# Last residual of the first half in tiles of its own, half of layer 1's v in products of 512 columns, and the last product with final_g by VectorE

## The chip, the cores and the metric

The kernel runs on one core of one Trainium2 chip. The metric is the device time of one launch in microseconds (us), the median of several runs. The engines are PE (TensorE: matrix products), ACT (ScalarE), DVE (VectorE), POOL (GpSimd) and SP (SyncE, whose queue issues all the transfers here). Each engine works through its own queue in order; an instruction waits until what it needs is done, and all that stands behind it on that engine waits with it.

## The reference

A trunk of two layers over 1024 tokens of 1024 channels, in fp32. Layer 0 has two mixers (a recurrent one, a, and a chunked attention, b), whose gated outputs go through one output projection; layer 1 has a gated product in which v is normalized over its channels and mixed over positions.

```python
def even_layer(h, ...):                       # layer 0
    p = rmsnorm(h, g) @ w_in
    ...
    y_a = rwkv7_mix(...) * silu(gate_a)       # 512 channels
    y_b = chunk_attention(...) * silu(gate_b) # 512 channels
    return h + concatenate([y_a, y_b]) @ w_out

def spatial_gating(u, v, ...):
    mu, var = mean(v), mean(square(v - mu))   # over the 1024 channels of a token
    v = (v - mu) * rsqrt(var + LN_EPS) * ln_g + ln_b
    sv = einsum('gij,bnjgc->bnigc', w, v in blocks of 128 tokens) + sg_b
    return u * sv

def odd_layer(h, ...):                        # layer 1
    u, v, gate = split(rmsnorm(h, g) @ w_in)  # 1024 columns each
    y = spatial_gating(gelu(u), gelu(v), ...)
    return h + (y * silu(gate)) @ w_out

def reference(x, ...):
    return rmsnorm(odd_layer(even_layer(x)), final_g)
```

## The kernel before

Every fp32 product is made of three products of rounded parts: an operand is cast to a high part (ACT) and the rest is subtracted out as a low part (POOL or DVE); `mm3_steps` then issues high × high (L256), high × low or low × high (L258), and the third (L260) for each of 8 (or 4) blocks of 128 contracted channels. Names with h or H are high parts, with l or L low ones. Tokens come in 8 blocks t of 128.

The program is written in one order and a scheduler, which simulates the engines, chooses from it the order of each engine's queue; buffers of a pool come round under a tag, and an instruction that takes a buffer again waits until its last reader is done.

Three places matter.

- **The output projection of layer 0** (`out_steps`, L1115). For a block t it loads y (`yraw`, L1123), casts it to `yh` (ACT, L1126), subtracts `yl` (L1127, DVE or POOL), and for each half n of 512 columns multiplies into one of two accumulators `acc` and adds the residual (DVE, L1142). It is made in two halves. The first, over `ya_d`, is in `fill_steps` and is fed between the steps of the attention: its residual is x, loaded into one of three buffers under the tag `res` (L1135), and the sum is stored in `hp_d` (L1167). The second, over `yb_d`, starts when the attention is done: for t = 0 the residual is `hp_d`, loaded through the same three `res` buffers; for later t it comes in `ht` (L1204). `wh` and `wl` of L222 and L225 are the first weights of layer 1, cast and subtracted meanwhile.
- **v of layer 1** (L1229 to L1241). v has 1024 columns in four blocks cb of 256. For each cb and t one product `accv` of 128 tokens × 256 columns (24 matmuls, with `xH2`, `xL2`, the normalized input, as the stationary operand) is evicted by ACT through gelu into `vp[cb][:, t]` (L1240), with its sum in `sv`. Behind it the mean `mu` is formed (DVE), 32 squares `junk` on ACT (L1263) give the variance, a reciprocal root of 8 columns on DVE follows (L72 to L85), then `v_norm` (L1274), the cast `vh` (ACT, L1289), the rest `vl` (POOL, L1290), and the products `psv` with the position weights (L1308, L1309). Meanwhile PE makes `accu` and `accg`, the u and gate products of layer 1. The weights of the output projection of layer 1, `WHL`, are loaded (L1112), cast (ACT, L1113) and subtracted (L1114) wherever the scheduler places them.
- **The end** (L1318 to L1355): for each t the output projection of layer 1, the sum of squares of each half (`junk`, ACT, L1341), `hg` = h × final_g for each half (POOL, L1342), the mean `v` (DVE, L1344), the reciprocal root (`rsqa`, `rstd`), the scaling of one half by DVE (L1347) and of the other by ACT (L1348), and the store.

Of the kernel before, what the change touches and what calls it, by code (L numbers as in the profile page):

```python
# [8 lines left out]
F32 = mybir.dt.float32  # L9
F32R = mybir.dt.float32r  # L10
I32 = mybir.dt.int32
BF16 = mybir.dt.bfloat16
AF = mybir.ActivationFunctionType
ALU = mybir.AluOpType
# [4 lines left out]
P = 128  # L19
T = 1024  # L20
D = 1024
KO = 8
# [41 lines left out]
def f32(ap):  # L64
    return ap.bitcast(F32)
# [34 lines left out]
def trunk_kernel(  # L100
# [4 lines left out]
    nc = tc.nc  # L105
    x = x[0]
# [90 lines left out]
    ya_d = dtile("ya_d", [NPAIR, P, T])  # L197
# [66 lines left out]
    def mm3(*args):  # L264
        run(mm3_steps(*args))
# [12 lines left out]
    ps_acc = pa.enter_context(tc.tile_pool(name="ps_acc", bufs=2, space=PSUM))  # L278
# [260 lines left out]
    for p in range(NPAIR):  # L539
# [23 lines left out]
        for hf in range(2):  # L563
            tsl = slice(hf * 512, hf * 512 + 512)
            psl = slice(p * P, p * P + P)
            r, k, v = rT[hf], kT[hf], vT[hf]
# [549 lines left out]
    def out_steps(t, ps_o, src, k0, parts, resid, ht, hp, yp, yb_, hi=nc.scalar.copy, lo=nc.vector):  # L1116

        tok = slice(t * P, t * P + P)
        yh, yl = [], []
        k1 = 0  # L1120
        for i, nk in enumerate(parts):
            raw = yp.tile([P, nk, P], F32, tag=f"yraw{i}", name="yraw", bufs=yb_)
            nc.sync.dma_start(raw, src[k1:k1 + nk, :, tok].rearrange("k p c -> p k c"))  # L1123
            h_ = yp.tile([P, nk, P], F32R, tag=f"yh{i}", name="yh", bufs=yb_)
            l_ = yp.tile([P, nk, P], F32R, tag=f"yl{i}", name="yl", bufs=yb_)
            hi(h_, raw)  # L1126
            lo.tensor_tensor(l_, raw, f32(h_), op=ALU.subtract)  # L1127
            yh += [h_[:, k] for k in range(nk)]
            yl += [l_[:, k] for k in range(nk)]
            k1 += nk  # L1130
        for n in range(2):
            ns = slice(512 * n, 512 * n + 512)
            if resid is not None:
                xt = hp.tile([P, 512], F32, tag="res", name="res", bufs=3)
                nc.sync.dma_start(xt, resid(t)[:, ns])  # L1135
            else:
                xt = ht[n]
            ps = ps_o.tile([P, 512], F32, tag="acc", name="acc")
            yield from mm3_steps(ps, lambda k: yh[k], lambda k: yl[k],
                                 lambda k: W[k0 + k][0][:, ns], lambda k: W[k0 + k][1][:, ns], k1)  # L1140
            ht[n] = xt if ht[n] is None else ht[n]
            nc.vector.tensor_tensor(ht[n], ps, xt, op=ALU.add)  # L1142
            yield
# [6 lines left out]
    def fill_steps():  # L1150

        nonlocal op
        yield from early
        pw.close()
        pf_.close()
        for k in range(KO):
            place_wout(xp, f"x{k}")
        op = po_.enter_context(tc.tile_pool(name="op", bufs=1, side="right"))
        yeng = (nc.gpsimd.tensor_copy if YP else nc.scalar.copy, nc.gpsimd if YP else nc.vector)
        weng = (nc.gpsimd.tensor_copy if WP else nc.scalar.copy, nc.gpsimd)  # L1160
        for c in range(4):
            load_wout(op, w_out_e[0], c, 2, *weng)
        for t in range(8):
            ht = [None, None]
            yield from out_steps(t, ps_acc, ya_d, 0, [4], lambda t: x[t * P:(t + 1) * P, :], ht, op, op, 2, *yeng)
            for n in range(2):
                nc.sync.dma_start(hp_d[t][:, 512 * n:512 * n + 512], ht[n])  # L1167
            if t < 4:
                load_wout(op, w_out_e[0], 4 + t, 2, *weng)

    op = None
# [22 lines left out]
    wpv = ExitStack()  # L1194
# [31 lines left out]


    sv = lp.tile([P, 4, 8], F32, name="sv")
    for c2 in range(2):  # L1229
        ws = [wv.pop() if wv else load_w(wvs[i], w_in_o[0], 1024 + 256 * (2 * c2 + i), n=256, bufs=1, rp=wvs[0])  # L1230
              for i in range(2)]
        for i, t4 in [(0, 0), (1, 0), (0, 1), (1, 1)]:
            cb = 2 * c2 + i
            wh, wl = ws[i]
            for t in range(4 * t4, 4 * t4 + 4):
                ts_ = slice(t * P, t * P + P)
                ps = ps_v.tile([P, 256], F32, tag="acc", name="accv")
                mm3(ps, lambda k: xH2[k][:, ts_], lambda k: xL2[k][:, ts_],
                    lambda k: wh[:, k, :], lambda k: wl[:, k, :])
                nc.scalar.activation(vp[cb][:, t], ps, AF.Gelu_apprx_tanh,  # L1240
                                     accum_out=sv[:, cb, t:t + 1])  # L1241
    wpv.close()
    lq = ctx.enter_context(tc.tile_pool(name="lq", bufs=1, side="right", reuse_waits="tile"))
    Rb = lq.tile([P, 8, P], F32, name="Rb")
# [82 lines left out]
    with tc.tile_pool(name="op1", bufs=1, reuse_waits="tile") as op:  # L1327
        fg = op.tile([P, D], F32, name="fg")
        nc.sync.dma_start(fg, final_g.unsqueeze(0).to_broadcast([P, D]))
        for t in range(8):  # L1330
# [5 lines left out]
            for n in range(2):  # L1336
                ns = slice(512 * n, 512 * n + 512)
                for _ in range(3 * KO):
                    next(steps)
                junk = op.tile([P, 512], BF16, tag="junk", name="junk", bufs=2)  # L1340
                nc.scalar.activation(junk, ht[:, ns], AF.Square, scale=D ** -0.5, accum_out=ms[:, n:n + 1])  # L1341
                nc.gpsimd.tensor_tensor(hg[:, ns], ht[:, ns], fg[:, ns], op=ALU.mult)  # L1342
            v = op.tile([P, 1], F32, tag="v", name="v", bufs=2)
            nc.vector.scalar_tensor_tensor(v, ms[:, 0:1], 1e-6, ms[:, 1:2], op0=ALU.add, op1=ALU.add)  # L1344
            rstd = op.tile([P, 1], F32, tag="rstd", name="rstd", bufs=2)
# [41 lines left out]
```

## Time and profile before

| | us |
|---|---|
| median of three runs | 1177.39 (1175.95, 1177.39, 1180.84) |
| the profiled execution | 1180.27, at a mean granted clock of 0.974 |
| its span in the trace | 1178.6 |
| PE busy | 1119.8 (95%) |
| DVE / ACT / POOL busy | 622.6 / 469.0 / 432.0 |
| bytes moved | 156.39 MB, mean 133 GB/s |

A row of the timeline is: start, length, engine, line, operation, output <- input, shape, and in brackets how long the engine had stood idle before it and what ended that. "x2" means two instructions in one row. A row of the chain is: start, length, what. Times in rows are counted from the start of the span. A matmul's length in a row is from its start until it has drained; the next one starts earlier than that, so the distance of two starts is what a matmul costs PE.

### The profile page before, as it was taken

How to read it: one execution, taken by the hardware profiler on the slowest of the kernel's cores; microseconds unless marked ns; L12 is line 12 of the kernel's file. 1: busy time of each engine (PE TensorE's matmuls, PEld its weight loads, DVE VectorE, ACT ScalarE, POOL GpSimd, SP SyncE). 2: the span in 40 equal slices, each digit the busy share in tenths (PEclk: the TensorE clock that was granted, in tenths of full speed). 3: DMA queues.
4: the chain of work that ended last, by engine and by line, in shares of the span. 5: the costliest groups of instructions: out<-in, count | busy, mean ns of one | idle time of the engine just before them, and what ended most of it. 6: DMA issues, size and time to landing. Idle time of an engine off the chain costs nothing.

```text
span 1178.6 us, 21117 instructions
## 1 busy us (share of the span) xinstructions
PE 1119.8 (95%) x8162; PEld 929.2 (79%) x8162; DVE 622.6 (53%) x1276; ACT 469.0 (40%) x1008; POOL 432.0 (37%) x448
## 2 busy tenths in 40 slices
PE   8999999998899898999997899899999999999997
PEld 5788778787777676767886778789998888888886
DVE  6455656456585867634687767464100753333433
ACT  5554554430322232312675646234417232231432
POOL 4345545361223433423322463311402464351222
PEclk9999999995999998999999899999999999999999
DMA  6124446469322533293587784862401232122541
GB/s 209 39 81 143 116 117 164 140 205 193 109 83 83 161 101 100 73 215 118 162 227 184 222 264 147 270 216 90 134 10 55 87 110 72 63 88 89 166 133 71
DMA packets 169125, 156.39 MB, mean 133 GB/s; under 512 B 25257, under 2 KB 138562, under 8 KB 168898
## 3 DMA queue, kind: packets, MB, share of 16 engines
q1 hardware_dynamic: 169026, 155.06, 44.9%
q8 instruction: 64, 1.05, 0.4%
q14 instruction: 35, 0.29, 0.1%
HBM read 102.02 MB, written 53.00 MB: 132 GB/s over the span
## 4 chain that ended last, share of the span: by engine, by line
PE 58%; DMA 7%; DVE 5%; ACT 1%; issue 1%; POOL 1%; SPq 0%; DVEq 0%; ACTq 0%; POOLq 0%
PE acc L256 8%; PE acc L258 8%; PE acc L260 8%; PE accv L256 3%; PE accv L260 3%; PE accv L258 3%; PE accu L256 3%; PE accu L260 2%; PE accg L260 2%; PE accu L258 2%; PE accg L258 2%; PE accg L256 2%; PE st L1069 2%; DMA wraw<-in_w_out_e_dram 2%; PE psx L770 1%; PE psg L713 1%
## 5 line engine op out<-in xcount | busy, mean ns | idle before, releaser
L256 PE MATMUL acc<-xH,wh 128*128 128x512 f32 x528 | 214.7, 407 | 1.6 <-DVE rT L422 0.6
L258 PE MATMUL acc<-xL,wh 128*128 128x512 f32 x528 | 213.5, 405 | 0.0
L225 POOL TENSOR_TENSOR wl<-wraw,wh 128x512 fp32r<-128x512 f32 (+1 forms) x106 | 148.9, 1424 | 175.4 <-ACT wh L222 160.0
L260 PE MATMUL acc<-xH,wl 128*128 128x512 f32 x528 | 212.0, 401 | 0.0
L256 PEld LDWEIGHTS acc<-xH,wh 128*128 128x128 f32 x528 | 101.5, 192 | 23.6 <-DVE rT L422 1.0
L258 PEld LDWEIGHTS acc<-xL,wh 128*128 128x128 f32 x528 | 101.2, 192 | 21.2 <-issue 0.9
L260 PEld LDWEIGHTS acc<-xH,wl 128*128 128x128 f32 x528 | 101.0, 191 | 21.2
L256 PE MATMUL acc<-WHL,yh 128*128 128x512 f32 x256 | 101.9, 398 | 4.5 <-DVE res L1142 3.4
L222 ACT CAST wh<-wraw 128x512 fp32r<-128x512 f32 (+1 forms) x102 | 62.7, 653 | 108.5 <-PE acc L258 43.3
L258 PE MATMUL acc<-WHL,yh 128*128 128x512 f32 x256 | 100.8, 394 | 0.0
L260 PE MATMUL acc<-WHL,yl 128*128 128x512 f32 x256 | 100.8, 394 | 0.0
L256 PE MATMUL accv<-wh,xH 128*128 128x256 f32 x256 | 71.7, 283 | 0.0
L258 PE MATMUL accv<-wl,xH 128*128 128x256 f32 x256 | 71.7, 283 | 0.0
L260 PE MATMUL accv<-wh,xL 128*128 128x256 f32 x256 | 71.4, 285 | 0.0
L256 PEld LDWEIGHTS acc<-WHL,yh 128*128 128x128 f32 x256 | 48.4, 189 | 15.6 <-DVE res L1142 4.1
L258 PEld LDWEIGHTS acc<-WHL,yh 128*128 128x128 f32 x256 | 48.3, 189 | 9.6 <-POOL WHL L1114 0.2
L260 PEld LDWEIGHTS acc<-WHL,yl 128*128 128x128 f32 x256 | 48.1, 188 | 9.7
L256 PE MATMUL accu<-xH,wh 128*128 128x512 f32 x128 | 50.5, 395 | 0.0
L260 PE MATMUL accu<-xH,wl 128*128 128x512 f32 x128 | 49.9, 390 | 0.0
L258 PE MATMUL accu<-xL,wh 128*128 128x512 f32 x128 | 49.9, 390 | 0.0
L260 PE MATMUL accg<-xH,wl 128*128 128x512 f32 x128 | 49.9, 389 | 0.0
L256 PE MATMUL accg<-xH,wh 128*128 128x512 f32 x128 | 49.8, 389 | 0.0
(433 smaller groups left out, 2438.0 us busy)
## 6 DMA issues: line engine op xcount, KB each, us to landing
wraw<-in_w_in_e_dram SPq DMA_DIRECT2D x66, 256.0 KB
wraw<-in_w_in_o_dram SPq DMA_DIRECT2D x32, 256.0 KB
xt<-in_x_dram SPq DMA_DIRECT2D x8, 512.0 KB
ar_d<-ar SPq DMA_DIRECT2D x8, 512.0 KB
q_d<-hl SPq DMA_DIRECT2D x8, 512.0 KB
bk<-bk_d SPq DMA_DIRECT2D x8, 512.0 KB
ag<-ar_d SPq DMA_DIRECT2D x16, 256.0 KB
k_d<-hl SPq DMA_DIRECT2D x8, 512.0 KB
```

The costliest lines, as they stand in the source:

```text
L222: c_ = hi(wh[:, ks], raw)
L225: nc.gpsimd.tensor_tensor(wl[:, ks], raw, f32(wh[:, ks]), op=ALU.subtract)
L256: fill(nc.tensor.matmul(ps, lhsT=ah(k), rhs=bh(k), start=(k == 0), stop=False), k == 0)
L258: fill(nc.tensor.matmul(ps, lhsT=ah(k), rhs=bl(k), start=False, stop=False), False)
L260: fill(nc.tensor.matmul(ps, lhsT=al(k), rhs=bh(k), start=False, stop=(k == nk - 1)), False)
L713: nc.tensor.matmul(psg[h][:, 2 * j + i], lhsT=bk[hss[h], 2 * pj + j, i, :], rhs=ag[hss[h], h, 2 * pj + j, i, :], start=True, stop=True)
L770: nc.tensor.matmul(ps[t_, i], lhsT=lhsT(f, i), rhs=rhs[f[0], i], start=True, stop=True)
L1069: nc.tensor.transpose(st[:, o:o + P], pfs[j][:, k0:k0 + P], ident)
```

## The change

It has three parts.

1. The two residual halves of t = 7 of the first half get buffers of their own (`res7`), under the tag `wraw` of the pool `op`, in which the raw output weights lay; they are loaded ahead of t = 5. The other residuals keep the three `res` buffers.
2. The second half of v (columns 512 to 1023 of v) is made in products of 512 columns: its weights lie in `wh2` and `wl2`, loaded in four pieces through the same raw buffers, and one product fills a whole accumulator, which ACT evicts in two pieces of 256. The first half of v stays in products of 256.
3. For t = 7 and n = 1 the product with final_g is made by DVE.

Where the order of the queues differs: DVE around the residuals of t = 7 (in the order's names `res_7967` and `res_7969` are the new tiles). Before, from the sum of t = 6 to that of the second half's t = 0:

```order
L1142 TENSOR_TENSOR res<-acc,res 128x512
L1083 TENSOR_TENSOR yb<-po,lo 64x512
L1142 TENSOR_TENSOR res<-acc,res 128x512 x2
L1127 TENSOR_TENSOR yl<-yraw,yh 128x512
L1142 TENSOR_TENSOR res<-acc,res 128x512 x2
L1127 TENSOR_TENSOR yl<-yraw,yh 128x512
L1142 TENSOR_TENSOR ht<-acc,res 128x512 x2
```

and in the changed kernel:

```order
L1145 TENSOR_TENSOR res<-acc,res 128x512
L1083 TENSOR_TENSOR yb<-po,lo 64x512
L1145 TENSOR_TENSOR res<-acc,res 128x512 x2
L1127 TENSOR_TENSOR yl<-yraw,yh 128x512
L1145 TENSOR_TENSOR res_7967<-acc,res_7967 128x512
L1145 TENSOR_TENSOR res_7969<-acc,res_7969 128x512
L1127 TENSOR_TENSOR yl<-yraw,yh 128x512
L1145 TENSOR_TENSOR ht<-acc,res 128x512 x2
```

The order is the same; only the two adds of t = 7 read other tiles. On SP the residual loads moved. Before, from the store of t = 5's second half on (`hp_d_132` is t = 0, `hp_d_139` t = 7):

```order
L1167 DMA hp_d_137<-res 128x512
L1135 DMA res<-in_x_dram 128x512
L1094 DMA yb_d<-yb 128x512
L1167 DMA hp_d_138<-res 128x512
L1123 DMA yraw<-yb_d 128x4x128
L221 DMA wraw<-in_w_in_o_dram 128x4x256 x2
L1167 DMA hp_d_138<-res 128x512
L1135 DMA res<-in_x_dram 128x512
L1123 DMA yraw<-yb_d 128x4x128
L1167 DMA hp_d_139<-res 128x512
L1135 DMA res<-hp_d_132 128x512
L221 DMA wraw<-in_w_in_o_dram 128x4x256
```

In the changed kernel the two loads of t = 7 stand some 20 rows earlier,

```order
L1175 DMA hp_d_135<-res 128x512
L1123 DMA yraw<-ya_d 128x4x128
L1172 DMA res_7967<-in_x_dram 128x512
L1172 DMA res_7969<-in_x_dram 128x512
L1175 DMA hp_d_135<-res 128x512
L1138 DMA res<-in_x_dram 128x512
L1123 DMA yraw<-ya_d 128x4x128
L990 DMA rd<-rr 4x128
L1138 DMA res<-in_x_dram 128x512
```

and at the place of before:

```order
L1175 DMA hp_d_137<-res 128x512
L1138 DMA res<-hp_d_132 128x512
L1094 DMA yb_d<-yb 128x512
L1175 DMA hp_d_138<-res 128x512
L1123 DMA yraw<-yb_d 128x4x128
L221 DMA wraw<-in_w_in_o_dram 128x4x256 x2
L1175 DMA hp_d_138<-res 128x512
L1138 DMA res<-hp_d_132 128x512
L1123 DMA yraw<-yb_d 128x4x128
L1175 DMA hp_d_139<-res_7967 128x512
L1175 DMA hp_d_139<-res_7969 128x512
```

The two residual loads of the second half (`res<-hp_d_132`) have moved up by one place each in the turn of the `res` buffers.

On ACT the casts of the output weights of layer 1 moved. Before, from the middle of v to the squares (`vp,sv<-accv` are the evictions of v):

```order
L1113 CAST WHL<-wraw 128x1024
L1240 ACTIVATE vp,sv<-accv 128x256 x2
L222 CAST wh<-wraw 128x1024 x2
L1113 CAST WHL<-wraw 128x1024
L1240 ACTIVATE vp,sv<-accv 128x256 x4
L222 CAST wh<-wraw 128x1024 x2
L1240 ACTIVATE vp,sv<-accv 128x256 x12
L222 CAST wh<-wraw 128x512 x2
L1240 ACTIVATE vp,sv<-accv 128x256 x2
L222 CAST wh<-wraw 128x512 x2
L1240 ACTIVATE vp,sv<-accv 128x256 x2
L1263 ACTIVATE junk,va_9745<-vp,mu 128x256 x10
```

and, at the end of v and in the squares, in the changed kernel:

```order
L1244 ACTIVATE vp,sv<-accv 128x256 x16
L1286 ACTIVATE junk,va_9547<-vp,mu 128x256 x4
L1113 CAST WHL<-wraw 128x1024
L1286 ACTIVATE junk,va_9547<-vp,mu 128x256 x2
L1113 CAST WHL<-wraw 128x1024
L1286 ACTIVATE junk,va_9547<-vp,mu 128x256
L1320 ACTIVATE y<-accu 128x512
L1286 ACTIVATE junk,va_9547<-vp,mu 128x256 x6
L1113 CAST WHL<-wraw 128x1024
L1286 ACTIVATE junk,va_9547<-vp,mu 128x256 x2
L1325 ACTIVATE th<-accg 128x512
L1286 ACTIVATE junk,va_9547<-vp,mu 128x256 x7
```

Before, three casts of WHL stood among the evictions of v and none among the 32 squares; now three stand among the squares. In the place of the former stand the casts of `wh2`. The load that they need on SP is issued behind a wait for the last product of v, because the new `wl2` lies where the raw output weights will. On PE the first `psv` stands 161 matmuls behind the last of v, where it stood 141 behind.

At the end DVE has one instruction more, the product of L1365, between the last add (L1145) and the mean `v` (L1368); on POOL 15 products with final_g are left of 16.

```diff
--- before.py
+++ after.py
@@ -1131,8 +1131,11 @@
         for n in range(2):
             ns = slice(512 * n, 512 * n + 512)
             if resid is not None:
-                xt = hp.tile([P, 512], F32, tag="res", name="res", bufs=3)
-                nc.sync.dma_start(xt, resid(t)[:, ns])
+                if isinstance(resid(t), list):
+                    xt = resid(t)[n]
+                else:
+                    xt = hp.tile([P, 512], F32, tag="res", name="res", bufs=3)
+                    nc.sync.dma_start(xt, resid(t)[:, ns])
             else:
                 xt = ht[n]
             ps = ps_o.tile([P, 512], F32, tag="acc", name="acc")
@@ -1160,9 +1163,14 @@
         weng = (nc.gpsimd.tensor_copy if WP else nc.scalar.copy, nc.gpsimd)
         for c in range(4):
             load_wout(op, w_out_e[0], c, 2, *weng)
+        res7 = []
         for t in range(8):
             ht = [None, None]
-            yield from out_steps(t, ps_acc, ya_d, 0, [4], lambda t: x[t * P:(t + 1) * P, :], ht, op, op, 2, *yeng)
+            if t == 5:
+                for n in range(2):
+                    res7.append(op.tile([P, 512], F32, tag="wraw", name="res7", bufs=2))
+                    nc.sync.dma_start(res7[n], x[7 * P:8 * P, 512 * n:512 * n + 512])
+            yield from out_steps(t, ps_acc, ya_d, 0, [4], lambda t: res7 if t == 7 else x[t * P:(t + 1) * P, :], ht, op, op, 2, *yeng)
             for n in range(2):
                 nc.sync.dma_start(hp_d[t][:, 512 * n:512 * n + 512], ht[n])
             if t < 4:
@@ -1226,19 +1234,34 @@
 
 
     sv = lp.tile([P, 4, 8], F32, name="sv")
-    for c2 in range(2):
-        ws = [wv.pop() if wv else load_w(wvs[i], w_in_o[0], 1024 + 256 * (2 * c2 + i), n=256, bufs=1, rp=wvs[0])
-              for i in range(2)]
-        for i, t4 in [(0, 0), (1, 0), (0, 1), (1, 1)]:
-            cb = 2 * c2 + i
-            wh, wl = ws[i]
-            for t in range(4 * t4, 4 * t4 + 4):
-                ts_ = slice(t * P, t * P + P)
-                ps = ps_v.tile([P, 256], F32, tag="acc", name="accv")
-                mm3(ps, lambda k: xH2[k][:, ts_], lambda k: xL2[k][:, ts_],
-                    lambda k: wh[:, k, :], lambda k: wl[:, k, :])
-                nc.scalar.activation(vp[cb][:, t], ps, AF.Gelu_apprx_tanh,
-                                     accum_out=sv[:, cb, t:t + 1])
+    def v_block(cb, n, t, wh, wl):
+
+        ts_ = slice(t * P, t * P + P)
+        ps = ps_v.tile([P, n * 256], F32, tag="acc", name="accv")
+        mm3(ps, lambda k: xH2[k][:, ts_], lambda k: xL2[k][:, ts_],
+            lambda k: wh[:, k, :], lambda k: wl[:, k, :])
+        for i in range(n):
+            nc.scalar.activation(vp[cb + i][:, t], ps[:, 256 * i:256 * i + 256], AF.Gelu_apprx_tanh,
+                                 accum_out=sv[:, cb + i, t:t + 1])
+
+    ws = [wv.pop() if i == 0 else load_w(wvs[1], w_in_o[0], 1024 + 256 * i, n=256, bufs=1, rp=wvs[0])
+          for i in range(2)]
+    wvs.append(wpv.enter_context(tc.tile_pool(name="wv2", bufs=1, reuse_waits="tile")))
+    wh2, wl2 = (wvs[2].tile([P, KO, 512], F32R, name=n) for n in ("wh2", "wl2"))
+    for i in range(2):
+        cs_ = slice(256 * i, 256 * i + 256)
+        for j in range(2):
+            ks = slice(4 * j, 4 * j + 4)
+            raw = wvs[0].tile([P, 4, 256], F32, tag="wraw", name="wraw", bufs=2)
+            nc.sync.dma_start(raw, w_in_o[0][:, 1536 + 256 * i:1792 + 256 * i].rearrange(
+                "(k p) c -> p k c", p=P)[:, ks])
+            nc.scalar.copy(wh2[:, ks, cs_], raw)
+            nc.gpsimd.tensor_tensor(wl2[:, ks, cs_], raw, f32(wh2[:, ks, cs_]), op=ALU.subtract)
+    for i, t4 in [(0, 0), (1, 0), (0, 1), (1, 1)]:
+        for t in range(4 * t4, 4 * t4 + 4):
+            v_block(i, 1, t, *ws[i])
+    for t in range(8):
+        v_block(2, 2, t, wh2, wl2)
     wpv.close()
     lq = ctx.enter_context(tc.tile_pool(name="lq", bufs=1, side="right", reuse_waits="tile"))
     Rb = lq.tile([P, 8, P], F32, name="Rb")
@@ -1339,7 +1362,8 @@
                     next(steps)
                 junk = op.tile([P, 512], BF16, tag="junk", name="junk", bufs=2)
                 nc.scalar.activation(junk, ht[:, ns], AF.Square, scale=D ** -0.5, accum_out=ms[:, n:n + 1])
-                nc.gpsimd.tensor_tensor(hg[:, ns], ht[:, ns], fg[:, ns], op=ALU.mult)
+                (nc.vector if t == 7 and n else nc.gpsimd).tensor_tensor(
+                    hg[:, ns], ht[:, ns], fg[:, ns], op=ALU.mult)
             v = op.tile([P, 1], F32, tag="v", name="v", bufs=2)
             nc.vector.scalar_tensor_tensor(v, ms[:, 0:1], 1e-6, ms[:, 1:2], op0=ALU.add, op1=ALU.add)
             rstd = op.tile([P, 1], F32, tag="rstd", name="rstd", bufs=2)
```

## The prediction

> **What bounds the kernel now.** First the page: the busy times, then the chain that ended last. Then the stretches around the places that the change touches.
>
> ```profile
> PE 1119.8 (95%) x8162; PEld 929.2 (79%) x8162; DVE 622.6 (53%) x1276; ACT 469.0 (40%) x1008; POOL 432.0 (37%) x448
> ...
> PE 58%; DMA 7%; DVE 5%; ACT 1%; issue 1%; POOL 1%; SPq 0%; DVEq 0%; ACTq 0%; POOLq 0%
> ```
>
> Then a table of three stretches (busy time of PE, PEld, DVE, ACT and POOL, then the granted clock, the DMA share and GB/s):
>
> ```profile
> 700.00:787.00 87.00, 80.43 (x400) 65.77 (x399) 55.15 (x144) 34.62 (x77) 29.71 (x24) 1.00 0.69 220
> 787.00:1171.00 384.00, 384.00 (x2145) 335.86 (x2143) 132.97 (x244) 128.97 (x296) 127.76 (x82) 1.00 0.29 92
> 829.15:893.73 64.58, 64.58 (x544) 64.58 (x543) 3.63 (x5) 20.39 (x59) 19.35 (x10) 1.00 0.25 79
> ```
>
> PE (TensorE) is busy 95% of the span and is most of the chain that ended last. From 787 to 1171 us it is busy for all of the 384 us, at a granted clock of 1.00. In that stage only fewer or shorter matmuls help, and a new wait costs in full. From 700 to 787 us PE lacks 6.6 us, so there a wait can be removed. After 1171 us only the tail is left.
>
> **Part 1: the residual of the last token block.** Two of the holes of that stretch are just ahead of the second half of the output projection. The rows are from the chain, then from the timeline of PE, DVE, ACT and POOL.
>
> ```profile
> 743.99 8.29 DMA res<-in_x_dram
> ...
> 756.03 0.02 issue
> ```
>
> ```profile
> 749.62 0.39 PE L260 MATMUL acc<-WHL,yl 128*128 128x512 f32 x1
> 753.21 0.50 PE L256 MATMUL acc<-WHL,yh 128*128 128x512 f32 x1 [3.20 <-DVE res L1142]
> 756.68 0.47 PE L256 MATMUL acc<-WHL,yh 128*128 128x512 f32 x1 [0.44 <-ACT yh L1126]
> 742.50 0.69 DVE L1127 TENSOR_TENSOR yl<-yraw,yh 128x512 fp32r<-128x512 f32 x1
> 744.61 0.69 DVE L1142 TENSOR_TENSOR res<-acc,res 128x512 f32<-128x512 f32 x1 [1.43 <-PE acc L260]
> 752.46 0.69 DVE L1142 TENSOR_TENSOR res<-acc,res 128x512 f32<-128x512 f32 x1 [7.16 <-DMA res<-in_x_dram]
> 753.07 2.87 DVE L1127 TENSOR_TENSOR yl<-yraw,yh 128x512 fp32r<-128x512 f32 x1
> 755.86 0.68 DVE L1142 TENSOR_TENSOR ht<-acc,res 128x512 f32<-128x512 f32 x1
> 749.55 1.05 ACT L222 CAST wh<-wraw 128x1024 fp32r<-128x1024 f32 x1 [7.22 <-DMA wraw<-in_w_in_o_dram]
> 751.88 0.61 ACT L1126 CAST yh<-yraw 128x512 fp32r<-128x512 f32 x1
> 750.68 4.71 POOL L225 TENSOR_TENSOR wl<-wraw,wh 128x1024 fp32r<-128x1024 f32 x2 [10.17 <-ACT wh L222]
> ```
>
> The last residual load of the first half is issued only at 743.99, when a res buffer comes free, and takes 8.29 us. DVE (VectorE) waits 7.16 us for it, and PE, which has two accumulators, waits for DVE. A matmul follows the one before after 0.227 us (rows further down), so PE would have gone on at 749.62 + 0.23 = 749.85: the hole is 3.36 us. The second, ahead of 756.68, follows from the next add, at 755.86, which stood behind the 2.87 us of yl on DVE: in the chain PE's work ahead of it ends at 756.03, so it is 0.65 us. Both together, 4.0 us, are the most that part 1 can bring.
>
> With tiles of its own the load is issued some 30 us earlier, behind the y load of t=5 on SP's queue. Both adds of t=7 then go as their products end: at 744.61 as now, and 2.72 us later. PE runs through the next product to 749.85 + 2.72 = 752.57. What is late next is the add of the product before it. By the order it stands on DVE behind yl of the next block, and yl waits for ACT's yh, which ends at 752.49 and keeps its place behind the two casts of wh. So yl is ready at about 752.55, and its length decides. Normally it takes 0.69 us; at 753.07 it took 2.87, because POOL's second wl subtraction was running (4.71 us for two: the second from 753.03 to 755.39), and ended 0.55 us after it. An operation of DVE that waits while POOL is between two such subtractions does get in, as a later place shows:
>
> ```profile
> 942.02 2.40 POOL L1290 TENSOR_TENSOR vhl<-vp,vhl 128x1024 fp32r<-128x1024 f32 x1 [3.27 <-ACT vhl L1289]
> 942.33 2.63 DVE L1315 TENSOR_TENSOR y<-y,s__10095 128x512 f32<-128x512 f32 x1
> 944.37 3.01 POOL L225 TENSOR_TENSOR wl<-wraw,wh 128x512 fp32r<-128x512 f32 x2
> ```
>
> There DVE's y waited for the POOL operation that ended at 944.42, ran, and POOL's next pair took 3.01 us. So here yl, waiting from 752.55, runs after the first subtraction, from 753.03 to about 753.65; the add ends 0.68 later, at 754.33, and PE goes on at 754.4 instead of 756.68. Part 1 is worth 2.3 us. If yl misses the moment again, it is worth nothing, since the add comes at 755.86 as now. The trace makes the miss a matter of 0.5 us: yl started less than 0.1 us after the second subtraction.
>
> The cost: two loads of 256 KB go in front of a store, a res load, a y load and a small one on SP. At the 220 GB/s of the stretch 700 to 787 us they are worth 2.4 us of delay at most, nothing at least. PE's other waits in that stretch end on ACT and DVE, none directly on a transfer; the longest group is this one:
>
> ```profile
> PE po L1074 <- ACT ph L1071: 2.1, 2, 1.5
> ```
>
> So I take nothing, and keep 2.4 us for the range. In turn, the two res loads of the second half move up into the slots of the removed ones, from after 751 to 740 and 744 us.
>
> **Part 2: 384 products of 256 columns become 192 of 512.** The 829.15 to 893.73 row gives the old pitch: 544 matmuls of 256 columns, two of which only touch the edges, so 64.58 / 542 = 0.1192 us. The new pitch comes from a product of 512 columns without a wait:
>
> ```profile
> 1168.01 0.39 PE L260 MATMUL acc<-WHL,yl 128*128 128x512 f32 x1
> 1170.73 0.39 PE L260 MATMUL acc<-WHL,yl 128*128 128x512 f32 x1
> ```
>
> Twelve steps in 2.72 us, 0.2267 us each. So 384 × 0.1192 = 45.77 us becomes 192 × 0.2267 = 43.53: a gain of 2.24 us, on PE's full stretch, thus on the path. (The mean lengths of one matmul would mislead here, since matmuls overlap.)
>
> The Trainium skill, page "TensorE: Matmul & The Clock Gate", section "Back-to-back issue gap", gives a spacing of N/2.4 + 2.5 ns, where halving the count saves only 2.5 ns each: an estimate of 192 × 2.5 ns = 0.5 us in place of 2.24. The trace differs: its 119 and 227 ns are 10 and 11 ns above that formula's, and the trace decides.
>
> The weights come in time. Their four casts and subtractions stand in the place of others that now end at 843, and they are needed when half of v is done, at 893.73 − 45.77 = 848 us. ACT still evicts 32 pieces of 256 columns, now two for each product, and each product takes twice as long. What the change moves is what stood there: the five loads of the output weights of layer 1. They must wait for memory that the last product of v reads, so they are issued at v's end E instead of 64 us earlier, and three of their casts go into ACT's 32 squares. The rows of before, from the timelines of SP, ACT, POOL, DVE and PE:
>
> ```profile
> 829.32 8.74 SPq L1112 DMA_DIRECT2D wraw<-in_w_out_o_dram  x4
> 833.08 1.05 ACT L1113 CAST WHL<-wraw 128x1024 fp32r<-128x1024 f32 x1 [2.95 <-DMA wraw<-in_w_out_o_dram]
> 838.36 4.75 POOL L225 TENSOR_TENSOR wl<-wraw,wh 128x1024 fp32r<-128x1024 f32 x2 [1.74 <-ACT wh L222]
> 895.03 0.51 ACT L1263 ACTIVATE junk<-vp,mu 128x256 bf16<-128x256 f32 x1 [0.50 <-DVE mu L1258]
> 913.44 0.17 DVE L1267 TENSOR_TENSOR va<-va,va 128x8 f32<-128x8 f32 x1 [5.29 <-ACT junk L1263]
> 913.64 0.17 DVE L1268 TENSOR_SCALAR va<-va 128x8 f32<-128x8 f32 x1
> 918.94 3.60 DVE L1274 TENSOR_SCALAR vp<-vp,mu,vr 128x256 f32<-128x256 f32 x8
> 922.58 2.00 ACT L1289 CAST vhl<-vp 128x1024 fp32r<-128x1024 f32 x2 [5.31 <-DVE vp L1274]
> 923.71 4.75 POOL L1290 TENSOR_TENSOR vhl<-vp,vhl 128x1024 fp32r<-128x1024 f32 x2 [3.58 <-ACT vhl L1289]
> 926.05 0.40 PE L1308 MATMUL psv<-wT,vhl 128*128 128x256 f32 x2
> ```
>
> Now the squares end at 913.4, E + 19.7. Changed: three casts of 1.05, and for the first a wait of about 0.8 us (a load lands 3.76 us after issue, 833.08 − 829.32, and only four squares stand ahead of it) make E + 23.7; with a wait before the third I take E + 25.4. Behind them 13 small operations of DVE at 0.2, now without one of PE's evictions between, 2.7 us, then the norm of 3.6 us and the first vh of 1.04: E + 32.7. PE reaches psv, by its new order, after 161 matmuls, E + 36.5. So 3.8 us are left, where before 923.6 against 926.05 left 2.4. Cost: nothing. If two loads took 8.29 us, as the one at 743.99 did, the squares would slip by 2 × (8.29 − 3.76) = 9.0, and PE would wait 9.0 − 3.8 = 5.2 us.
>
> **Part 3: the last product by DVE.**
>
> ```profile
> 1152.12 0.15 DVE L1344 SCALAR_TENSOR_TENSOR v<-ms 128x1 f32<-128x1 f32 x1
> 1171.16 0.69 DVE L1142 TENSOR_TENSOR ht<-acc,res 128x512 f32<-128x512 f32 x1 [4.79 <-PE acc L260]
> 1171.94 0.63 ACT L1341 ACTIVATE junk<-ht 128x512 bf16<-128x512 f32 x1 [4.76 <-DVE ht L1142]
> 1171.93 1.26 POOL L1342 TENSOR_TENSOR hg<-ht,fg 128x512 f32<-128x512 f32 x1 [4.13 <-DVE ht L1142]
> 1172.70 0.51 DVE L1344 SCALAR_TENSOR_TENSOR v<-ms 128x1 f32<-128x1 f32 x1 [0.85 <-ACT junk L1341]
> ```
>
> In the tail POOL's product makes v last 0.51 us where it takes 0.15 elsewhere. On DVE the product, as long as the add of the same size, 0.69, runs from 1171.85 to 1172.54 under ACT's square. v starts at 1172.70 as before and ends 0.36 earlier, on the path. Bounds: a gain of 0.36; a loss of 0.2 if the product runs past 1172.70.
>
> **The sum.** −2.3 − 2.24 − 0.36 = −4.9 us. The profiled execution took 1180.27 (span 1178.6 and 1.67 around it), so it would take 1175.4. It is 2.88 above the median of the runs, 1177.39; there the sum gives 1172.5. Part of those 2.88 may be the wait for the late load itself, so I round to 1172.7. Some 0.5%, 5.9 us here, is what a measurement of this kernel can tell from no change: the forecast lies just inside it.
>
> **The rivals.** (a) yl misses POOL's pause: −2.6, 1174.8. For it: 0.5 us decide; against it: yl is no longer behind the late add. (b) Both holes close, if the casts of wh move and yl is early: −4.0 − 2.24 − 0.36 = −6.6, 1170.8. Against it: yh's time is set by loads that this change leaves alone. (c) The time of a matmul goes by its columns alone, and two of 256 cost as much as one of 512: part 2 is worth nothing, −2.66, 1174.7; both measured pitches speak against it. The Trainium skill's formula, named above, is close to this: by it the sum would be −3.2, 1174.2. (d) Slower: the output weights, late behind v's end, hold ACT's squares up. It decides from 3.8 us of slip on, costs 1 us for each, and has eaten the gain at 3.8 + 4.9 = 8.7 us; with the 9.0 us above it ends at 1177.7, and with two loads of 11 us each (a slip of 14.6), at 1183.3. Against it: a DMA share of 0.29 there, against 0.69 where a load took 8.29. (e) The first part does nothing, since the two loads of t=7 hold up others by the 2.4 us: as (a), 1174.9.
>
> **How the numbers follow.** The forecast 0.55, (a) 0.14, (b) 0.13, (c) 0.03, (d) 0.09, (e) 0.06. The executions before differ by 4.9 us, so each case is good to about 1.5 us in a median. Faster by over 0.5% (under 1171.5): most of (b) and a third of the forecast, 0.31. Slower by over 0.5% (above 1183.3): half of (d) and a little for what I did not see, 0.07. The rest, 0.62. The range reaches from (b) less its scatter, 1168.8, to (a) and the mild end of (d), 1177.2.
>
> **What would show it.** Part 1: no DVE wait on a residual near 752; PE's wait at 753.21 gone, one of about 1.8 us ahead of 754.4 left. Part 2: a pitch of 0.227 in the last 192 products of v, and psv without a wait. Part 3: v at 0.15 us. Wrong it would be by a PE wait ahead of psv, a new one between 710 and 740 us, or weights of the second half of v that come after it begins.

## The result and the profile after

| | before | changed |
|---|---|---|
| median of 21 runs each, us | 1180.53 (1175.95 to 1184.03) | 1173.73 (1168.11 to 1177.90) |
| ratio | | 0.995, 95% interval 0.9935 to 0.9965 |
| profiled execution: span, us | 1178.6 | 1172.1 |

The change makes the kernel about 5.9 us faster (4.1 to 7.7), where 4.7 against the median then known, 4.9 by the sum, was forecast. Single runs of one kernel differ by up to 17 us, and much of that goes with TensorE's granted clock: over the 71 runs of the kernel before that were made beside the experiments, time and mean clock go together with a correlation of −0.85, and within all the kernels here a run is 9.1 us shorter for each 0.01 of clock. (Two more, of 1323.64 and 6066.05 us, count as slow and are left out everywhere.) So below, besides ratios, stands a mean *at the same clock*: each run moved along that line to 0.975, with its standard error. Before is at 1177.2 ± 0.2 in those 71 runs (of its 21 in the table the clock was not recorded), the changed kernel at 1172.4 ± 0.4: 4.8 ± 0.4 us less. This is a help and no proof: the runs lie on several chips, and where a wait makes the clock fall, as one below does, the correction takes part of its cost away.

The page of the changed kernel's profile:

```profile
span 1172.1 us, 20750 instructions
...
PE 1117.2 (95%) x7970; PEld 919.2 (78%) x7970; DVE 620.3 (53%) x1277; ACT 468.3 (40%) x1008; POOL 432.6 (37%) x447
...
PE 58%; DMA 6%; DVE 6%; issue 2%; ACT 1%; POOL 1%; SPq 0%; DVEq 0%; POOLq 0%; ACTq 0%
```

192 matmuls are gone, and PE's share of the chain is what it was. Where the 6.5 us of span went is read from four marks on PE and one on DVE. In the timelines of before, the last product of the attention, the first and the last of v, and DVE's last scaling (the last matmul, at 1170.73, stands in the prediction):

```profile
735.70 0.39 PE L1076 MATMUL po<-pl,vb 128*128 128x384 f32 x2
...
787.77 0.28 PE L256 MATMUL accv<-wh,xH 128*128 128x256 f32 x1
...
893.73 0.28 PE L260 MATMUL accv<-wh,xL 128*128 128x256 f32 x1
...
1174.31 0.49 DVE L1347 TENSOR_SCALAR hg<-hg,rstd 128x512 f32<-128x512 f32 x1
```

The same in the changed kernel, with two rows more: the product at 758.24, which waits, and the first psv. (The bracket at 758.24 names a small DVE operation, rstd; the row of the add on DVE, further down, shows what the wait is for.)

```profile
734.48 0.39 PE L1076 MATMUL po<-pl,vb 128*128 128x384 f32 x2
...
758.24 0.47 PE L256 MATMUL acc<-WHL,yh 128*128 128x512 f32 x1 [1.04 <-DVE rstd L81]
...
783.85 0.28 PE L256 MATMUL accv<-wh,xH 128*128 128x256 f32 x1
...
887.48 0.39 PE L260 MATMUL accv<-wh,xL 128*128 128x512 f32 x1
...
924.42 0.40 PE L1331 MATMUL psv<-wT,vhl 128*128 128x256 f32 x2
...
1164.57 0.39 PE L260 MATMUL acc<-WHL,yl 128*128 128x512 f32 x1
...
1167.82 0.48 DVE L1371 TENSOR_SCALAR hg<-hg,rstd 128x512 f32<-128x512 f32 x1
```

Distances between the marks in the profiled executions, in us, of all kernels but the two with the shortest products (the last column from the last matmul's start to DVE's last scaling, L1347 in before):

| kernel | start to end of attention | to first of v | first to last of v | to last matmul | to last scaling |
|---|---|---|---|---|---|
| before | 735.7 | 52.07 | 105.96 | 277.00 | 3.58 |
| changed | 734.5 | 49.37 | 103.63 | 277.09 | 3.25 |
| part 1 alone | 733.5 | 49.27 | 105.99 | 277.00 | 3.58 |
| part 2 alone | 732.3 | 51.18 | 103.62 | 277.10 | 3.58 |
| part 3 alone | 731.1 | 50.86 | 105.99 | 277.00 | 3.25 |
| changed, halves of 256 | 734.0 | 50.64 | 106.26 | 277.02 | 3.25 |
| changed, t = 1 through res | 732.0 | 49.28 | 103.60 | 277.09 | 3.25 |
| changed, weights late | 728.2 | 47.85 | 103.63 | 277.09 | 3.25 |
| the same again | 733.9 | 47.84 | 103.60 | 277.10 | 3.24 |
| before, weights late | 735.3 | 51.77 | 105.98 | 277.00 | 3.59 |
| changed, again | 731.4 | 52.02 | 103.60 | 277.09 | 3.25 |

The last three columns repeat within 0.03 us for the same code: part 2 is worth 2.33 us there, part 3 0.33. The first column is what scatters (nothing in it is changed but two loads), so the 1.2 us that it gives to the 6.5 are no gain of the change that these profiles can show; the second is where part 1 acts, and scatters too.

Part 1 in the changed kernel, from the timelines of DVE, then POOL, then from the chain:

```profile
746.12 0.69 DVE L1145 TENSOR_TENSOR res<-acc,res 128x512 f32<-128x512 f32 x1 [2.03 <-PE acc L260]
749.61 1.12 DVE L1127 TENSOR_TENSOR yl<-yraw,yh 128x512 fp32r<-128x512 f32 x1 [2.80 <-ACT yh L1126]
750.65 0.68 DVE L1145 TENSOR_TENSOR ht<-acc,res 128x512 f32<-128x512 f32 x1
...
757.40 0.69 DVE L1145 TENSOR_TENSOR ht<-acc,ht 128x512 f32<-128x512 f32 x1 [3.10 <-DMA ht<-hp_d]
```

```profile
747.78 5.22 POOL L225 TENSOR_TENSOR wl<-wraw,wh 128x1024 fp32r<-128x1024 f32 x2 [8.50 <-ACT wh L222]
```

```profile
751.20 6.11 DMA ht<-hp_d
```

The add of t = 7 waits for PE alone (746.12). yl gets in between POOL's two subtractions, which take 5.22 us instead of 4.71, and lasts 1.12 us instead of 2.87. Then a new wait: the add at 757.40 waits 3.10 us for the residual of t = 1, issued at 751.20 and landed 6.11 us later, and PE waits 1.20 us for that add, ahead of 758.24. In the chain that load's issue follows, on SP, a load of y that was held until yl had ended (749.61 + 1.12).

Part 2 behind v, from the timelines of ACT and DVE:

```profile
891.46 1.06 ACT L1113 CAST WHL<-wraw 128x1024 fp32r<-128x1024 f32 x1
...
919.13 2.00 ACT L1312 CAST vhl<-vp 128x1024 fp32r<-128x1024 f32 x2 [6.86 <-DVE vp L1297]
```

```profile
912.30 0.62 DVE L1290 TENSOR_TENSOR va<-va,va 128x8 f32<-128x8 f32 x1 [0.82 <-ACT junk L1286]
...
916.42 2.68 DVE L1297 TENSOR_SCALAR vp<-vp,mu,vr 128x256 f32<-128x256 f32 x8
```

The squares end at 912.3, 24.8 us behind the last product of v at 887.48, and psv starts 36.9 behind it, without a wait. Part 3, DVE's timeline:

```profile
1165.72 0.69 DVE L1365 TENSOR_TENSOR hg<-ht,fg 128x512 f32<-128x512 f32 x1
1166.54 0.16 DVE L1368 SCALAR_TENSOR_TENSOR v<-ms 128x1 f32<-128x1 f32 x1
```

### The profile page after: what moved, and what is told of

Same layout as the page of the kernel before. It is cut to its first block, busy times and chain, and to the rows that moved or that the text cites. A ratio compares the mean times of both kernels' runs of the same rounds, so it can differ in the third digit from the quotient of the medians.

```text
span 1172.1 us, 20750 instructions
## 1 busy us (share of the span) xinstructions
PE 1117.2 (95%) x7970; PEld 919.2 (78%) x7970; DVE 620.3 (53%) x1277; ACT 468.3 (40%) x1008; POOL 432.6 (37%) x447
## 4 chain that ended last, share of the span: by engine, by line
PE 58%; DMA 6%; DVE 6%; issue 2%; ACT 1%; POOL 1%; SPq 0%; DVEq 0%; POOLq 0%; ACTq 0%
PE acc L256 7%; PE acc L258 7%; PE acc L260 7%; PE accv L256 3%; PE accv L260 3%; PE accv L258 3%; PE accu L256 3%; PE accu L260 2%; PE accu L258 2%; PE accg L258 2%; PE accg L260 2%; PE accg L256 2%; PE st L1069 2%; PE psx L770 1%; DMA wraw<-in_w_out_e_dram 1%
## 5 line engine op out<-in xcount | busy, mean ns | idle before, releaser
L225 POOL TENSOR_TENSOR wl<-wraw,wh 128x512 fp32r<-128x512 f32 (+1 forms) x102 | 140.5, 1395 | 139.9 <-ACT wh L222 127.6
L222 ACT CAST wh<-wraw 128x512 fp32r<-128x512 f32 (+1 forms) x98 | 58.6, 635 | 107.9 <-PE acc L258 39.7
L256 PE MATMUL accv<-wh,xH 128*128 128x256 f32 (+1 forms) x192 | 60.5, 319 | 0.0
L258 PE MATMUL accv<-wl,xH 128*128 128x256 f32 (+1 forms) x192 | 60.5, 319 | 0.0
L260 PE MATMUL accv<-wh,xL 128*128 128x256 f32 (+1 forms) x192 | 60.2, 321 | 0.0
L1114 POOL TENSOR_TENSOR WHL<-wraw,WHL 128x512 fp32r<-128x512 f32 (+1 forms) x20 | 30.1, 1506 | 66.2 <-ACT WHL L1113 65.5
```

The source lines that it names most:

```text
L222: c_ = hi(wh[:, ks], raw)
L225: nc.gpsimd.tensor_tensor(wl[:, ks], raw, f32(wh[:, ks]), op=ALU.subtract)
L256: fill(nc.tensor.matmul(ps, lhsT=ah(k), rhs=bh(k), start=(k == 0), stop=False), k == 0)
L258: fill(nc.tensor.matmul(ps, lhsT=ah(k), rhs=bl(k), start=False, stop=False), False)
L260: fill(nc.tensor.matmul(ps, lhsT=al(k), rhs=bh(k), start=False, stop=(k == nk - 1)), False)
L1114: (lo or (nc.vector if k % 2 else nc.gpsimd)).tensor_tensor(wl, raw, f32(wh), op=ALU.subtract)
```

## The experiments

**Each part alone.** Part 1 alone is the diff's first three pieces on the kernel before; part 2 alone its fourth; part 3 alone its last.

> Part 1 alone (the residuals of t = 7 in tiles of their own, all else as before). If the late residual load was the cause of both holes: the 3.4 us hole ahead of the product that follows t = 7 goes, the second shrinks, and a new wait of about 1.2 us for the load of hp_d of t = 1 stays, as in the changed kernel: 2.3 to 2.7 us off between the start of the second half and v, v itself unchanged at 45.8 us for its second half. Time 1.0 to 4 us below before in the median (the scatter of single runs is 4 us). Rival (the gain of the first stretch is run-to-run scatter, or comes with part 2's order): holes as before, time unchanged.

Measured: ratio 0.9982 (0.9961 to 1.0003); at the same clock 2.2 ± 0.6 us below before. The stretch to v takes 49.27 us, as expected, and the one wait left is the new one:

```profile
757.14 0.47 PE L256 MATMUL acc<-WHL,yh 128*128 128x512 f32 x1 [1.17 <-DVE rstd L81]
```

> Part 2 alone (second half of v in products of 512 columns). If the pitch of matmuls is the cause: the last 192 products of v take 43.5 us where 384 took 45.8, psv without a wait of PE, both holes near 750 us still there; time about 2.3 us below before. Rival (two matmuls of 256 cost as much as one of 512 and what helps is that the loads of the output weights leave the stage): the second half of v takes 45.8 us or more.

Measured: ratio 0.9976 (0.9952 to 1.0000); at the same clock 3.7 ± 0.6 us below before, more than the 2.3 that the marks show; where the rest comes from is not shown (in the profile it lies ahead of v, where this part changes nothing). v takes 103.62 us. The late residual is still there, from DVE's timeline:

```profile
747.06 0.69 DVE L1142 TENSOR_TENSOR res<-acc,res 128x512 f32<-128x512 f32 x1 [5.16 <-DMA res<-in_x_dram]
747.66 2.49 DVE L1127 TENSOR_TENSOR yl<-yraw,yh 128x512 fp32r<-128x512 f32 x1
```

but it is 2 us earlier than in the profile of before, and PE's hole 1.35 us instead of 3.36; in the profile of part 3 alone, where this place is as before too, it is 1.58. The hole that the prediction read from one execution was a long one.

> Part 3 alone (the last product with final_g by DVE). If POOL's product held up DVE's v: from the start of the last matmul to the end of the span 0.3 to 0.4 us less than before, v 0.16 us long instead of 0.51; the span as a whole within its scatter. Rival (DVE's product delays v): v starts later than 1.97 us after the last matmul's start, and nothing is gained.

Measured: one execution, 1174.18 us, span 1172.5. From the last matmul to the last scaling 3.25 us instead of 3.58; DVE's timeline:

```profile
1166.13 0.69 DVE L1342 TENSOR_TENSOR hg<-ht,fg 128x512 f32<-128x512 f32 x1
1166.95 0.16 DVE L1345 SCALAR_TENSOR_TENSOR v<-ms 128x1 f32<-128x1 f32 x1
```

v is 0.16 us long, and it starts 1.97 us behind the last matmul (at 1164.98) as in before (1172.70 − 1170.73). The rival falls.

**Is it the matmul pitch?** The same tiles, loads and evictions, with shorter matmuls:

```diff
         ps = ps_v.tile([P, n * 256], F32, tag="acc", name="accv")
-        mm3(ps, lambda k: xH2[k][:, ts_], lambda k: xL2[k][:, ts_],
-            lambda k: wh[:, k, :], lambda k: wl[:, k, :])
+        for i in range(n):          # halves of 256; in the next two runs quarters of 128, eighths of 64
+            c_ = slice(256 * i, 256 * i + 256)
+            mm3(ps[:, c_], lambda k: xH2[k][:, ts_], lambda k: xL2[k][:, ts_],
+                lambda k: wh[:, k, c_], lambda k: wl[:, k, c_])
```

> The changed kernel, but each product of 512 columns of v's second half is made as two of 256 into the two halves of the same accumulator: same tiles, loads, casts, evictions and moved output weights, only the matmuls are 384 again. If the pitch of matmuls is the cause: the second half of v takes 45.8 us again, parts 1 and 3 stay, time about 3 us below before, 2.3 above the changed kernel. Rival (the gain of v comes from the moved loads and casts): v's second half stays at 43.5 us and the time at the changed kernel's, 6 us below before.

Measured: ratio 0.9994 (0.9978 to 1.0010); at the same clock 0.7 ± 0.5 us below before. v takes 106.26 us, 2.63 more than with 512 columns: the gain of part 2 is the matmuls', and the moved loads bring none. What is left is less than the 3 us expected, and the profile shows a reason for part of it. Timelines of ACT, POOL, DVE and PE:

```profile
745.45 1.05 ACT L222 CAST wh<-wraw 128x1024 fp32r<-128x1024 f32 x1 [4.78 <-DMA wraw<-in_w_in_o_dram]
747.55 1.05 ACT L222 CAST wh<-wraw 128x1024 fp32r<-128x1024 f32 x1 [1.04 <-DMA wraw<-in_w_in_o_dram]
```

```profile
746.58 4.76 POOL L225 TENSOR_TENSOR wl<-wraw,wh 128x1024 fp32r<-128x1024 f32 x2 [7.75 <-ACT wh L222]
```

```profile
749.15 2.74 DVE L1127 TENSOR_TENSOR yl<-yraw,yh 128x512 fp32r<-128x512 f32 x1 [2.79 <-ACT yh L1126]
```

```profile
752.64 0.47 PE L256 MATMUL acc<-WHL,yh 128*128 128x512 f32 x1 [1.57 <-DVE ht L1145]
```

This is rival (a) of the prediction: the second weight load landed later, the second cast began 2.10 us after the first instead of 1.35, so yh came when POOL's second subtraction had begun (746.58 + 2.38), yl took 2.74 us, and PE waited 1.73 us. The stretch takes 50.64 us instead of 49.37.

> The changed kernel, but each 512 columns of v's second half made as four products of 128 columns into the same accumulator, 768 matmuls in place of 192. If a matmul costs its columns plus a fixed part, as 0.1192 and 0.2267 us for 256 and 512 give (0.42 ns a column and 11.7 ns): 0.0655 us each, second half of v 50.3 us, 6.8 above the changed kernel's 43.5. Rival (for short products the load of the stationary operand, 128 columns for each, becomes the bound): clearly more than 0.0655 each, 0.08 us or above, 62 us or more.

Measured: ratio 1.0326 (1.0294 to 1.0358); v takes 145.92 us, 42.3 more than with 512, so its second half 85.8. My account falls, the rival holds. PE's timeline, 18 steps from the first row to the last:

```profile
879.84 0.28 PE L260 MATMUL accv<-wh,xL 128*128 128x128 f32 x1
...
881.85 0.27 PE L260 MATMUL accv<-wh,xL 128*128 128x128 f32 x1
```

0.1117 us each, hardly less than 0.1192 for twice the columns.

> The changed kernel, but each 512 columns of v's second half as eight products of 64 columns, 1536 matmuls. With 128 columns a matmul cost 0.1117 us, hardly less than the 0.1192 of 256. If this is the load of the stationary operand, the same for every product: again 0.11 us each, second half of v some 171 us, span about 1172 + 128 = 1300 us. Rival (a dearer column below 256, and 128 x 0.87 ns): 0.056 to 0.06 us each, second half as with 128 columns, 86 to 92 us.

Measured: one execution of 1454.16 us. PE's timeline, 36 steps from the first row to the second, then three, and two rows of the table of stretches:

```profile
842.18 0.28 PE L260 MATMUL accv<-wh,xL 128*128 128x64 f32 x1
...
846.20 0.28 PE L260 MATMUL accv<-wh,xL 128*128 128x64 f32 x1
...
1000.19 0.40 PE L260 MATMUL accv<-wh,xL 128*128 128x64 f32 x1
...
1000.83 0.40 PE L260 MATMUL accv<-wh,xL 128*128 128x64 f32 x1
```

```profile
842.00:846.00 4.00, 4.00 (x39) 4.00 (x37) 0.17 (x1) 0.98 (x3) 1.27 (x1) 1.00 0.68 211
900.00:950.00 50.00, 50.00 (x236) 50.00 (x236) 0.00 (x0) 0.84 (x4) 0.00 (x0) 0.50 0.00 0
```

For the first 4 us these products run at full clock and take 0.1117 us each, as those of 128 columns do. Then the granted clock falls to 0.50 and stays there until they end, at 0.213 us each. So a matmul with a new stationary operand of 128 columns takes 0.112 us at full clock, whether it moves 128 columns or 64, as the account of the load of that operand says; the weight loads (PEld, the second busy time in a row) leave no gap in either row. That it is the load and no other fixed cost of such a pair is argued, not shown, since no run changed the size of the stationary operand. The fall of the clock, which neither account expected, made it nearly twice as dear. With 256 columns (0.1192) this floor is still close; of the sizes tried only 512 (0.2267) is clear of it. The Trainium skill, page "TensorE: Matmul & The Clock Gate", section "LDWEIGHTS (loading the stationary operand)", gives columns / 1.2 ns for such a load, an estimate of 107 ns for 128 columns; the 112 measured here are 5 above it. The Trainium skill, page "TensorE: Matmul & The Clock Gate", section "Back-to-back issue gap", does not fit these runs: its formula, given there for an isolated matmul, comes to 56 ns for 128 columns, and it names 81 ns as what a stream of such pairs sustains.

**What is left of part 1's wait.** Two ways to take away the wait for t = 1's residual. The first changes one constant, `HRT = 1` to `HRT = 2` (the first t whose residual comes in `ht`).

> The changed kernel, with the residual of t = 1 of the second half also loaded in halves through the res buffers, as t = 0's is, so that its load no longer stands on SP behind a weight load that waits for POOL. If the 1.2 us wait of PE ahead of t = 2 of the second half is that late load: it goes or shrinks below 0.4 us, time about 1 us below the changed kernel's. Rival (the transfers of that stretch share one bandwidth, which is at 0.9 of the DMA engines there, and another load comes late in its place): the wait moves to t = 2 or t = 3 and the time stays.

Measured: ratio 0.9953 (0.9935 to 0.9971), as the changed kernel; the stretch 49.28 us. The rival holds: the wait went to t = 2. PE's and DVE's timelines:

```profile
761.21 0.47 PE L256 MATMUL acc<-WHL,yh 128*128 128x512 f32 x1 [1.07 <-DVE rstd L73]
```

```profile
760.37 0.69 DVE L1145 TENSOR_TENSOR ht<-acc,ht 128x512 f32<-128x512 f32 x1 [2.48 <-DMA ht<-hp_d]
```

The second holds the first weights of layer 1 back on SP:

```diff
-            nc.sync.dma_start(h_d[t], ht)
-            if t == WVT:
-                wv = [load_w(wvs[0], w_in_o[0], 1024, n=256, bufs=1)]
+            st = nc.sync.dma_start(h_d[t], ht)
+            if t == 1:
+                wv = [load_w(wvs[0], w_in_o[0], 1024, n=256, bufs=1, ld=st)]
```

where `ld` makes each load of raw weights follow that store in SP's order.

> The changed kernel, with the loads of v's first weights held back on SP until the store of t = 1 of the second half (they are needed when v begins, some 25 us later), and with them ACT's casts and POOL's subtractions. If what is left of PE's waits there (1.3 us in the changed kernel, moved to t = 2 in the run with t = 1's residual in res buffers) comes from these 2 MB crowding the residuals: from the last product of the attention to the first of v 48.1 us instead of 49.4, no PE wait over 0.3 us, and yl never meets POOL's subtraction; time some 1 us below the changed kernel's, 6 to 7 below before. Rival (another transfer takes their place, or the weights now come late): the wait moves on, to t = 2 to 4, or to the first product of v, and the stretch stays at 49.4 or grows.

Measured: ratio 0.9964 (0.9940 to 0.9988), 4.2 us below before where 6 to 7 were expected; the stretch 47.85 us with no wait of PE in it. All that PE waits for from 700 to 787 us, ahead of the stretch, from the view of the waits:

```profile
PE po L1078 <- DVE pl L1074: 0.5, 1, 0.5
```

DVE's adds (L1147 here) come one after the other as the products end, and SP issues the residuals of t = 1 and 2 early:

```profile
742.58 0.69 DVE L1147 TENSOR_TENSOR ht<-acc,res 128x512 f32<-128x512 f32 x1 [1.43 <-PE acc L262]
745.30 0.69 DVE L1147 TENSOR_TENSOR ht<-acc,res 128x512 f32<-128x512 f32 x1 [2.03 <-PE acc L262]
```

```profile
741.60 1.04 SPq L1214 DMA_DIRECT2D ht<-hp_d  x2
```

That is 13.4 us after the last product of the attention (728.22); in the changed kernel it is 16.7 (751.20 − 734.48). The profile says 1.5 us against the changed kernel, the ratio nothing. So it was run again beside the changed kernel on one chip.

> The changed kernel with v's first weights held back, a second time, beside the changed kernel itself on one chip. The first time its profile had no PE wait between attention and v (47.9 us against 49.4), but its median stood only 4 us below before, as if nothing were gained on the changed kernel. If the 1.5 us are real and the median was the scatter of the granted clock (a run's time falls by some 9 us for each 0.01 of clock): compared at the same clock 1 to 1.5 us below the changed kernel. Rival (what is saved there comes back later): no difference at the same clock.

> The changed kernel again, unchanged, on the same chip as the run before it: 4.5 to 5.5 us below before at the same clock; in the profile one PE wait of 1.0 to 1.5 us between attention and v, for the residual of t = 1.

Measured: weights late, ratio 0.9930 (0.9914 to 0.9946); changed kernel, 0.9966 (0.9945 to 0.9988). At the same clock, with all runs taken together, the version with late weights is at 1171.0 ± 0.5 (18 runs) and the changed kernel at 1172.9 ± 0.3 (32 runs): 1.9 ± 0.6 less, where 1 to 1.5 were expected. So this version beats both kernels, and that the first comparison showed no gain over the changed kernel lies within the scatter. The changed kernel itself misses what was expected of it: 3.6 ± 0.6 us below before at the same clock, not 4.5 to 5.5, and in its second profile a wait of 2.47 us, not 1.0 to 1.5. That profile shows what the wait can cost. PE's timeline and two rows of the table of stretches:

```profile
756.25 0.47 PE L256 MATMUL acc<-WHL,yh 128*128 128x512 f32 x1 [2.30 <-DVE rstd L81]
```

```profile
753.00:757.00 4.00, 1.70 (x8) 1.14 (x7) 1.48 (x5) 0.62 (x1) 1.26 (x1) 0.98 0.97 328
757.00:760.00 3.00, 3.00 (x8) 2.32 (x8) 1.71 (x5) 1.15 (x2) 0.00 (x0) 0.50 0.44 145
```

Here PE waited 2.47 us for the same residual, at a DMA share of 0.97, and soon after worked at half the clock for some 3 us: the stretch took 52.0 us, as long as before.

> The kernel before, with only the loads of v's first weights held back in the same way; the residuals of t = 7 still wait for a res buffer. If the late residual load was slow because of these weights (8.3 us for 256 KB) and not only because of its late issue: it lands within some 4 us, the first hole falls from 3.4 to below 1 us, the second goes since POOL is free, and the stretch from the attention's last product to v's first takes 48.5 to 49.5 us instead of 52.1; time 2.5 to 3.5 us below before. Rival (the late issue alone makes the hole): 51 us or more, time within 1 us of before.

The same edit on the kernel before. Measured: ratio 1.0009 (0.9983 to 1.0034); at the same clock 0.2 ± 0.6 us below before; the stretch 51.77 us. Half of each account holds. DVE's timeline (adds are L1144 here) and two rows of the table of stretches:

```profile
746.94 0.69 DVE L1144 TENSOR_TENSOR res<-acc,res 128x512 f32<-128x512 f32 x1 [2.03 <-PE acc L262]
...
759.08 0.69 DVE L1144 TENSOR_TENSOR ht<-acc,ht 128x512 f32<-128x512 f32 x1 [2.28 <-DMA ht<-hp_d]
```

```profile
757.00:760.00 3.00, 0.87 (x5) 0.44 (x4) 0.89 (x3) 0.62 (x1) 1.26 (x1) 1.00 0.98 355
760.00:764.00 4.00, 4.00 (x11) 3.12 (x12) 2.61 (x9) 1.15 (x2) 0.00 (x0) 0.59 0.64 179
```

With the weights out of the way the last residual, issued at its old, late place, was there in time, and both old holes are gone: the late issue alone did not make them. But the residual of t = 1 makes PE wait 2.29 us, and the clock falls for some 3 us soon after. From the chain:

```profile
747.56 3.35 DMA hp_d<-res
...
752.25 6.73 DMA ht<-hp_d
```

On SP its load stands behind a residual load that gets its res buffer only when that store has ended, at 750.91. So it is issued 16.9 us after the last product of the attention (735.31), and it takes 6.73 us, though the weights are issued only at 762.79; with weights on the way it took 6.11 and 7.45. So the version that loses this wait differs in when the load is issued; that the weights' transfers slow it is not shown. Part 1 takes the old residual loads out of its way, the late weights let yl and the load of y ahead of it go early; neither edit does it alone, both together do (13.4 us).

## Why the prediction was right, point by point

- **Sum and time.** −4.9 forecast; 5.9 (4.1 to 7.7) by ratio, 4.8 ± 0.4 at the same clock, 3.6 ± 0.6 in its second comparison, 4.4 ± 0.4 with all 32 runs. The time, 1172.7 forecast and 1173.73 measured, is that of the likeliest case, but the closeness is partly luck: the forecast started from 1177.39, the median of three runs, and 21 runs gave 1180.53; from there the sum of −4.9 leads to 1175.6. Against the 0.5% that was taken as the bound of no change, the first ratio lies on it (0.995) and the second inside (0.9966).
- **Part 1, −2.3: near in the profiled pair (−2.70), but made up otherwise, so that the agreement is partly luck; its size as a mean is open.** That the first hole goes held. The wait of 1.8 us ahead of the product behind it shrank to 0.12, since the casts came earlier than in the profile of before and yl got in at once. In its place came a wait of 1.20 us for the residual of t = 1, which the prediction did not name: it moved two loads up and did not ask what the load behind them waits for on SP, a load of y that waits for yl. Rival (a) was real: in the run with halves of 256 yl missed the pause. Over the profiles with part 1 and the weights in their old place the stretch takes 49.3 to 52.0 us (mean of the seven with the two runs of shorter products, 49.5 and 50.3: 50.0), without it 50.9 to 52.1 (mean of three 51.4): 1.3 us, give or take 0.5 by their spread; the runs of part 1 alone give 2.2 ± 0.6 at the same clock. The term was read from one execution whose hole was the longest of three.
- **Part 2, −2.24: right** (−2.33 us: 103.60 to 103.63 in the six profiles with it, 105.96 to 105.99 in the four without), for the pitches that the prediction took. Rival (c), and with it the formula of the Trainium skill, fell. That the moved weights cost nothing held to a few tenths: squares at E + 24.8 (25.4 forecast), the first vh at 919.13 + 1.05, E + 32.7 (32.7), psv at E + 36.9 (36.5). Rival (d) did not come (its larger slip, 14.6 us, should read 2 × (11 − 3.76) = 14.5).
- **Part 3, −0.36: right** (−0.33).
- **Loads of t = 7 ahead of others, rival (e):** no new wait of PE on a transfer between 700 and 740 us; the first column of the table shows no loss beyond its scatter.

## What to carry to other kernels

A hole in a full engine can come from a load that is issued too late or lands too slowly; here both occurred. What is not needed for another 25 us goes behind what is, and a residual moved up only helps until the next one behind it on the queue. A product that loads a new stationary operand for each matmul wants 512 moving columns; at 256 (0.1192 us) it is already near the floor of 0.112. Where a mean of many runs is not to be had, marks on the critical engine price a change to 0.03 us in stretches that PE fills, while one wait of one execution says little on its mean.

## What was not expected of the hardware

- With 64 moving columns per matmul the granted clock fell to 0.50 some 4 us after the first of them and stayed there through unbroken PE work (847 to 1165 us); with 128 it did not fall (1.00 from 860 to 920 us there).
- Waits of PE of 2.29 and 2.47 us were each followed by 3.3 us at half clock, which cost about 1.5 us more; waits of 3.36 and 1.98 us at nearly the same place were not. The Trainium skill, page "TensorE: Matmul & The Clock Gate", section "What's actually happening", tells of a free-running window of some 3.4 us over which activity is watched, and of a low clock after an idle one; the length of the slow spells agrees, and that some waits shorter than the window were enough is this case's finding.
- The run-to-run scatter of this kernel goes with that clock: 9.1 us for each 0.01 of its mean. In the profiles it lies ahead of the end of the attention, where the clock is 0.96 as a mean in before (0 to 735 us); from 787 to 1171 us it is 1.00.
